# Moving the weight rings of a two-layer hybrid encoder into an on-chip pool of their own

## The chip, the cores and the metric

The kernel runs on one core of a Trainium2 chip. The metric is device time in microseconds of one execution, the median of several runs. The kernel before took 982.03 us (median of 3 runs, 981.92 to 982.07).

## The reference

Two layers work on an input x of 256 rows by 1024 columns, all in float32. Each layer has a mixing part with four branches (attention with compressed keys and values, a short convolution, a convolution of 31 taps, and a gated block) and a feed-forward part:

```python
for l in range(DEPTH):                       # DEPTH = 2
    h = rms_norm(x, norm_mix_pre[l])
    proj = h @ w_in[l]                       # 1024 x 8224
    (c_q, c_kv, k_rope, sc_b, sc_c, sc_x, cf_a, cf_g, gm_u, gm_v, gate_logits) = jnp.split(proj, pts, axis=-1)
    y_a = mla_branch(...) @ w_o_mla[l]
    y_b = short_conv_branch(...) @ w_o_sc[l]
    y_c = conformer_branch(...) @ w_o_cf[l]
    y_d = gmlp_branch(...) @ w_o_gm[l]
    g = jax.nn.sigmoid(gate_logits.reshape(B, S, N_BRANCH, D) + gate_b[l])
    merged = g[:, :, 0] * y_a + g[:, :, 1] * y_b + g[:, :, 2] * y_c + g[:, :, 3] * y_d
    x = x + rms_norm(merged @ w_out[l], norm_mix_post[l])
    h2 = rms_norm(x, norm_ffn_pre[l])
    f_g, f_u = jnp.split(h2 @ w_ffn_in[l], 2, axis=-1)       # 1024 x 5632
    x = x + rms_norm((jax.nn.silu(f_g) * f_u) @ w_ffn_out[l], norm_ffn_post[l])
```

All weights together are 41.4 million float32 numbers, each used for 256 rows.

## The kernel before

**Weights.** The host lays all weights out as a list of units in the order of their use, 128 partitions by at most 2048 numbers (`unit_list`). A unit passes through three rings of buffers. `Weights.load` (lines 325 to 334) takes a buffer `raw` (4 of them, 128 x 2048 float32) and issues its DMA on the SP queue. `Weights.split` (lines 336 to 351) takes a buffer `hi` and a buffer `lo` (5 of each, 128 x 2048 of the type F32R, four bytes a number): ScalarE copies `raw` into `hi`, which rounds it, and VectorE subtracts `hi` from `raw` into `lo`, in pieces of 1024 columns.

**Products.** The activations are split into a pair in the same way (`hth`/`htl` for the normalized input, `fh`/`fl`, `mh`/`ml` and others). A product of float32 precision is three matmuls: high with high, and high with low both ways (`group`, line 381). In most products `hi` and `lo` are the moving operand, up to 512 columns a matmul, and the activations are the stationary one, 128 columns loaded into the array before each matmul. In `b_unit` (12 units per layer) it is the other way round: 128 columns of `hi` or `lo` are loaded as the stationary operand and `hth` or `htl` is moving, 256 columns in two pieces of 128.

**Order.** A planner inside the program (`Engine`, `issue`, `event`, `pump`) simulates the engines with cost formulas and so writes out the order of the instructions of ScalarE, VectorE, GpSimd and SP once, when the program is built; matmuls are in the order of the text. It knows tiles by name and by offset inside the tile; where a tile lies in on-chip memory does not enter it.

**Pools and addresses.** Tiles come from pools (lines 256 to 258): `cp` for what lives throughout, `sb` for everything that rotates, and `ps` for PSUM. Pools lie one behind the other in the order in which they are opened; in a pool the rings (one per tag) lie one behind the other in the order of first use, each buffer rounded up to a multiple of 32 bytes per partition. The program's own list of buffers gives these starts, in bytes per partition:

| buffer | start | remainder by 64 |
|---|---|---|
| hth, htl (in cp) | 27,712, 35,904 | 0 |
| ident (in cp) | 24,768 | 0 |
| end of cp, first gain of sb | 44,096 | 0 |
| raw, 4 x 8192 | 52,288 and on | 0 |
| slots of 512 numbers (fh, mh, wst, gv, f, pt and others), 25 x 2048 | 85,056 and on | 0 |
| pii (2 numbers) | 136,256 | 0 |
| fr and others of 16 numbers | 136,288 | 32 |
| h, y: "big", 2 x 4096 | 136,544 | 32 |
| one-number columns, 8 x 32 | 144,736 | 32 |
| hi, 5 x 8192 | 144,992 and on | 32 |
| lo, 5 x 8192 | 185,952 and on | 32 |
| two-number columns | 226,912 | 32 |

The tile `pii` takes 32 bytes, and so all rings that follow it start 32 bytes past a multiple of 64. Within a unit, a column slice that a matmul reads starts at a multiple of 64 bytes from the start of its buffer (512, 1024, 1088, 1536 or 2048 bytes).

Of the kernel before, what the change touches and what calls it, by code (L numbers as in the profile page):

```python
# [11 lines left out]
F32 = mybir.dt.float32  # L12
F32R = mybir.dt.float32r
# [5 lines left out]
P = 128  # L19
# [14 lines left out]
UW = 2048  # L34
# [62 lines left out]
def hybrid_encoder(ctx: ExitStack, tc: tile.TileContext, wts, x_in, pos, invf, cols, rows, wst, out):  # L97
# [156 lines left out]
    act, dve, pool, sp, pe = Engine(nc.scalar, "ACT", cost_act), Engine(nc.vector, "DVE", cost_dve), Engine(nc.gpsimd, "POOL", cost_pool), Engine(nc.sync, "SP", lambda *a: 0.1), Tensor()  # L254

    cp = ctx.enter_context(tc.tile_pool(name="cp", bufs=1))
    sb = ctx.enter_context(tc.tile_pool(name="sb", bufs=1))
    ps = ctx.enter_context(tc.tile_pool(name="ps", bufs=1, space=bass.MemoryType.PSUM))

    B_RAW, B_HI, B_SLOT, B_BIG, B_GAIN = 4, 5, 25, 2, 2  # L260
# [7 lines left out]
    def nm(s):  # L268
        cnt[0] += 1
        return f"{s}_{cnt[0]}"  # L270
# [36 lines left out]
    def load(dst, src, after=0.0):  # L307
        nc.sync.dma_start(dst, src)  # L308
        n = 4.0 * width(dst) * dst.shape[0]
        dma[0] = max(dma[0], clock[0] + 1.0, after + 1.0) + n / 400e3  # L310
        mark(done, region(dst), dma[0] + 1.8)
# [8 lines left out]
    class Weights:  # L320
# [4 lines left out]
        def load(self, i, t=0.0):  # L325
            l, u = divmod(i, NU)
            w, after = widths[u], t
            t = sb.tile([P, UW], F32, tag="raw", name=nm("raw"), bufs=B_RAW)
            o = (l * offs[-1] + offs[u]) * P
            src = wts[o : o + w * P].rearrange("(p w) -> p w", w=w)  # L330
            step = FIRST if i == 0 else w
            for c in range(0, w, step):
                load(t[:, c : c + step], src[:, c : c + step], after)
            self.raw[i] = t

        def split(self, i):
            w = widths[i % NU]
            h = sb.tile([P, UW], F32R, tag="hi", name=nm("hi"), bufs=B_HI)
            lo = sb.tile([P, UW], F32R, tag="lo", name=nm("lo"), bufs=B_HI)
            raw = self.raw.pop(i)  # L340
            step = FIRST if i == 0 else 1024
            self.parts[i] = (h, lo)
            spans = [(c, min(w, c + step)) for c in range(0, w, step)]

            def rank():
                return 0 if i <= self.n + NEAR else 3

            for c, e in spans:
                act.copy(h[:, c:e], raw[:, c:e], rank=rank)
                dve.tensor_tensor(lo[:, c:e], raw[:, c:e], h[:, c:e], op=ALU.subtract, rank=rank, then=self.more if e == w else None)  # L350
# [54 lines left out]
    def gain(l, i):  # L405
        g = sb.tile([P, D], F32, tag="gain", name=nm("gain"), bufs=B_GAIN)
        load(g, rows[l : l + 1, i * D : (i + 1) * D].partition_broadcast(P))
        return g

    def brow(l, i):  # L410
        g = slot(s="brow")
        o = 4 * D + 512 * i
        load(g, rows[l : l + 1, o : o + 512].partition_broadcast(P))
        return g

    def gate_row(l, gi, n):
        g = slot(s="brow")
        o = 4 * D + 4 * 512 + D * gi + 512 * n
        load(g, rows[l : l + 1, o : o + 512].partition_broadcast(P))
        return g  # L420
# [54 lines left out]
    def pre_norm(t, g):  # L475
        h = big()
        ss = small(1)
        r = small(1)
        act.activation(h, x[:, t, :], AF.Square, scale=D ** -0.5, accum_out=ss, rank=FAST)
        rstd_of(r, ss, rank=FAST)  # L480
        for j in range(2):
            c = slice(512 * j, 512 * (j + 1))
            dve.scalar_tensor_tensor(h[:, c], x[:, t, c], r, g[:, c], op0=ALU.mult, op1=ALU.mult, rank=FAST)

        def turn():
            for j in range(2):
                yield need(h)
                b = sbank()
                transposes(b, [h[:, 512 * j + P * k : 512 * j + P * (k + 1)] for k in range(4)])
                bv = b.rearrange("p (k n) -> p k n", n=P)  # L490
                split(hth[:, t, 4 * j : 4 * j + 4, :], htl[:, t, 4 * j : 4 * j + 4, :], bv, FAST)

        return turn()
# [83 lines left out]
    def layer(l):  # L577
# [26 lines left out]
        def mla_tr(t, cn):  # L604
            yield need(cn)
            b = sbank()
            transposes(b, [cn[:, P * k : P * (k + 1)] for k in range(4)])
            for j in range(2):
                o = slice(t * P, (t + 1) * P)
                split(ft2(qc[j])[:, :, o], ft2(ql[j])[:, :, o], b[:, 256 * j : 256 * (j + 1)].rearrange("p (f n) -> p f n", f=2))  # L610
# [84 lines left out]
        def split_op(name, j, src):  # L695
            hi, lo = slot(F32R, name + "h"), slot(F32R, name + "l")
            split(hi, lo, src)
            ops[name][j] = (ft2(hi), ft2(lo))
# [481 lines left out]
```

## Time and profile before

| | us |
|---|---|
| median of 3 runs | 982.03 |
| the profiled execution | 981.91 |
| its span, first to last instruction | 980.1 |
| TensorE busy (matmuls) | 966.4 |
| VectorE busy | 670.3 |
| ScalarE busy | 476.2 |

The page of the profile shows the busy time of each engine, the chain of work that ended last, and the costliest groups of instructions. Matmuls overlap in the records: the next one starts while the last is still draining, so the recorded length of one (about 0.39 us for 512 columns) is not what it adds to the time. What it adds is the distance from its start to the next one's start; the chain shows it as the length of a piece divided by the number of its matmuls. Names of a matmul stand as output<-moving,stationary, followed by the size of the stationary operand and that of the output.

### The profile page before, as it was taken

What the parts mean: (1) busy time and instruction counts of PE and PEld (TensorE: products, weight loads), DVE (VectorE), ACT (ScalarE), POOL (GpSimd) and SP (SyncE); (2) the same over time, 40 slices, a digit from 0 to 9 for tenths busy, and PEclk for the clock granted to TensorE, in tenths of its full rate; (3) what the DMA queues carried; (4) which work ended last, traced back from release to release, by engine and by line L of the source; (5) the groups of instructions that cost most, each with busy time, mean ns of one, the idle gap of its engine ahead of it and who ended that gap; (6) DMA issues with size and microseconds to landing.
All of it is one profiled execution on the core that took longest, in us unless ns stands there. A gap on an engine that the chain in (4) does not pass through costs nothing.

```text
span 980.1 us, 12950 instructions
## 1 busy us (share of the span) xinstructions
PE 966.4 (99%) x5098; PEld 818.5 (84%) x5098; DVE 670.3 (68%) x1018; ACT 476.2 (49%) x733; POOL 44.5 (5%) x87
## 2 busy tenths in 40 slices
PE   8999999999999999999999999999999999999997
PEld 7999988888887888888899999888888878888885
DVE  6969888888847655553387888779987485544532
ACT  6666645345435544443275655444455364444421
POOL 1100000000001000000031000000000110000000
PEclk9999999999999999999999999999999999999999
DMA  9844344565744655464267244455576275555501
GB/s 363 290 154 172 121 170 151 183 216 189 282 150 172 220 191 190 172 217 175 86 238 279 78 172 168 142 174 203 183 258 222 77 261 212 172 178 192 211 0 43
DMA packets 29726, 179.52 MB, mean 183 GB/s; under 512 B 3681, under 2 KB 3809, under 8 KB 10209
## 3 DMA queue, kind: packets, MB, share of 16 engines
q1 hardware_dynamic: 29664, 178.69, 51.1%
q8 instruction: 40, 0.66, 0.3%
q14 instruction: 22, 0.17, 0.0%
HBM read 177.63 MB, written 1.05 MB: 182 GB/s over the span
## 4 chain that ended last, share of the span: by engine, by line
PE 94%; DVE 2%; ACT 1%; issue 1%; DMA 1%; POOL 1%; SPq 0%; DVEq 0%; POOLq 0%; ACTq 0%
PE pb L248 74%; PE acc L248 13%; PE psd L252 4%; PE psd L248 2%; PE av L248 1%; DVE lo L175 1%; DMA raw<-in_wts_dram 1%; POOL c L175 1%; ACT hi L175 1%; DVE h L175 0%; ACT h L175 0%; DVE x L175 0%; SPq L308 0%; DVE htl L175 0%; ACT sq L175 0%
## 5 line engine op out<-in xcount | busy, mean ns | idle before, releaser
L175 DVE TENSOR_TENSOR lo<-raw,hi 128x1024 fp32r<-128x1024 f32 (+4 forms) x321 | 374.1, 1202 | 142.4 <-ACT hi L175 141.9
L175 ACT CAST hi<-raw 128x1024 fp32r<-128x1024 f32 (+4 forms) x321 | 318.6, 1035 | 287.9 <-PE pb L248 153.8
L248 PE MATMUL pb<-hi,hth 128*128 128x512 f32 (+1 forms) x704 | 275.7, 392 | 1.0 <-ACT hth L175 1.0
L248 PE MATMUL pb<-lo,hth 128*128 128x512 f32 (+1 forms) x704 | 271.5, 386 | 3.3 <-DVE lo L175 3.3
L248 PE MATMUL pb<-hi,htl 128*128 128x512 f32 (+1 forms) x704 | 271.6, 386 | 0.6 <-DVE htl L175 0.4
L248 PEld LDWEIGHTS pb<-lo,hth 128*128 128x128 f32 x704 | 132.2, 188 | 32.0 <-DVE lo L175 4.6
L248 PEld LDWEIGHTS pb<-hi,htl 128*128 128x128 f32 x704 | 132.0, 187 | 31.0 <-DVE htl L175 2.0
L248 PEld LDWEIGHTS pb<-hi,hth 128*128 128x128 f32 x704 | 132.1, 188 | 28.7 <-ACT hth L175 1.3
L248 PE MATMUL pb<-hth,hi 128*128 128x256 f32 x384 | 109.2, 284 | 0.0
L248 PE MATMUL pb<-hth,lo 128*128 128x256 f32 x384 | 107.9, 281 | 0.0
L248 PE MATMUL pb<-htl,hi 128*128 128x256 f32 x384 | 107.9, 281 | 0.0
L175 DVE SCALAR_TENSOR_TENSOR yc<-zc,hcol,yc 128x241 f32<-128x241 f32 (+14 forms) x240 | 97.7, 471 | 0.0
L248 PEld LDWEIGHTS pb<-htl,hi 128*128 128x128 f32 x384 | 72.4, 189 | 0.3
L248 PEld LDWEIGHTS pb<-hth,hi 128*128 128x128 f32 x384 | 72.4, 188 | 0.3
L248 PEld LDWEIGHTS pb<-hth,lo 128*128 128x128 f32 x384 | 72.4, 188 | 0.0
L248 PE MATMUL acc<-hi,fh 128*128 128x512 f32 x176 | 69.8, 396 | 0.0
L248 PE MATMUL acc<-hi,fl 128*128 128x512 f32 x176 | 69.5, 395 | 0.0
L248 PE MATMUL acc<-lo,fh 128*128 128x512 f32 x176 | 69.5, 395 | 0.0
L248 PEld LDWEIGHTS acc<-hi,fl 128*128 128x128 f32 x176 | 33.0, 187 | 8.0
L248 PEld LDWEIGHTS acc<-hi,fh 128*128 128x128 f32 x176 | 33.0, 188 | 8.0
L248 PEld LDWEIGHTS acc<-lo,fh 128*128 128x128 f32 x176 | 33.0, 188 | 7.9
L175 POOL TENSOR_SCALAR c<-c 128x1 f32<-128x1 f32 (+1 forms) x20 | 12.5, 626 | 530.6 <-ACT sq L175 486.8
(161 smaller groups left out, 1009.9 us busy)
## 6 DMA issues: line engine op xcount, KB each, us to landing
raw<-in_wts_dram SPq DMA_DIRECT2D x152, 1024.0 KB, 4.8
brow<-in_rows_dram SPq DMA_DIRECT2D x24, 256.0 KB, 5.2
gain<-in_rows_dram SPq DMA_DIRECT2D x8, 512.0 KB, 6.2
raw<-in_wts_dram SPq DMA_DIRECT2D x3, 816.0 KB, 4.5
raw<-in_wts_dram SPq DMA_DIRECT2D x2, 768.0 KB, 5.9
raw<-in_wts_dram SPq DMA_DIRECT2D x2, 544.0 KB, 6.1
x<-in_x_dram SPq DMA_DIRECT2D x2, 512.0 KB, 5.9
out_dram<-x SPq DMA_DIRECT2D x4, 256.0 KB, 2.1
```

What stands on the lines that cost most here:

```text
L175: o.emit = lambda: f(*a, **k)
L248: nc.tensor.matmul(out, lhsT, rhs, **k)
L252: nc.tensor.transpose(out=out, in_=in_, identity=identity)
```

## The change

A third pool for on-chip memory, `wp`, is opened between `cp` and `sb`, and the three weight rings `raw`, `hi` and `lo` take their buffers from it in place of `sb`. Number, size, type and tags of the buffers stay; no instruction, wait or queue is named in the diff.

```diff
     cp = ctx.enter_context(tc.tile_pool(name="cp", bufs=1))
+    wp = ctx.enter_context(tc.tile_pool(name="wp", bufs=1))
     sb = ctx.enter_context(tc.tile_pool(name="sb", bufs=1))
...
         def load(self, i, t=0.0):
...
-            t = sb.tile([P, UW], F32, tag="raw", name=nm("raw"), bufs=B_RAW)
+            t = wp.tile([P, UW], F32, tag="raw", name=nm("raw"), bufs=B_RAW)
...
         def split(self, i):
             w = widths[i % NU]
-            h = sb.tile([P, UW], F32R, tag="hi", name=nm("hi"), bufs=B_HI)
-            lo = sb.tile([P, UW], F32R, tag="lo", name=nm("lo"), bufs=B_HI)
+            h = wp.tile([P, UW], F32R, tag="hi", name=nm("hi"), bufs=B_HI)
+            lo = wp.tile([P, UW], F32R, tag="lo", name=nm("lo"), bufs=B_HI)
```

## Rows read from the trace of the kernel before

**Rows 1.** The page, first part: busy time, share of the span and instructions of each engine.

```profile
PE 966.4 (99%) x5098; PEld 818.5 (84%) x5098; DVE 670.3 (68%) x1018; ACT 476.2 (49%) x733; POOL 44.5 (5%) x87
...
PEclk9999999999999999999999999999999999999999
```

**Rows 2.** The page, fourth part: the chain that ended last, by engine and by line.

```profile
PE 94%; DVE 2%; ACT 1%; issue 1%; DMA 1%; POOL 1%; SPq 0%; DVEq 0%; POOLq 0%; ACTq 0%
PE pb L248 74%; PE acc L248 13%; PE psd L252 4%; PE psd L248 2%; PE av L248 1%; DVE lo L175 1%; DMA raw<-in_wts_dram 1%; POOL c L175 1%; ACT hi L175 1%; DVE h L175 0%; ACT h L175 0%; DVE x L175 0%; SPq L308 0%; DVE htl L175 0%; ACT sq L175 0%
```

**Rows 3.** Waits of TensorE: who waited for whom, us in total, times, longest.

```profile
PE pb L248 <- DVE lo L175: 3.3, 3, 1.5
```

**Rows 4.** The chain in order of time, four pieces: start us, us, what, instructions.

```profile
350.82 22.39 PE pb L248 x96
...
432.25 57.39 PE acc L248 x246
...
592.97 5.68 PE pb L248 x48
```

**Rows 5.** TensorE in order of time, 506 to 512 us, first and last of 48: start, us, form.

```profile
506.05 0.29 PE L248 MATMUL pb<-hi,hth 128*128 128x272 f32 x1
...
511.94 0.29 PE L248 MATMUL pb<-hi,htl 128*128 128x272 f32 x1
```

**Rows 6.** Matmul groups by shape: count | busy us, mean ns of one | idle before.

```profile
L248 PE MATMUL pb<-hi,hth 128*128 128x512 f32 x640 | 257.0, 402 | 0.0
...
L248 PE MATMUL pb<-hi,hth 128*128 128x272 f32 x64 | 18.7, 292 | 1.0 <-ACT hth L175 1.0
...
L248 PE MATMUL pb<-hth,hi 128*128 128x256 f32 x384 | 109.2, 284 | 0.0
...
L248 PE MATMUL acc<-hi,fh 128*128 128x512 f32 x176 | 69.8, 396 | 0.0
...
L248 PE MATMUL pb<-hi,mh 128*128 128x512 f32 x64 | 25.8, 403 | 0.0
...
L248 PE MATMUL pb<-hi,sch 128*128 128x512 f32 x32 | 13.2, 412 | 0.0
```

**Rows 7.** Groups of weight loads on TensorE, same columns.

```profile
L248 PEld LDWEIGHTS pb<-hi,hth 128*128 128x128 f32 x704 | 132.1, 188 | 28.7 <-ACT hth L175 1.3
...
L248 PEld LDWEIGHTS pb<-hth,hi 128*128 128x128 f32 x384 | 72.4, 188 | 0.3
```

**Rows 8.** TensorE in order of time: eight transposes of h, and what starts after.

```profile
504.05 1.03 PE L252 MATMUL psd<-ident,h 128*128 128x128 f32 x8
504.92 0.60 PE L252 MATMUL psd<-ident,cn 128*128 128x128 f32 x4
```

**Rows 9.** The chain, columns as in rows 4: eight transposes of f; 16 records of psd<-wst,gv.

```profile
349.95 0.87 PE psd L252 x8
...
72.60 1.78 PE psd L248 x16
```

**Rows 10.** VectorE and ScalarE groups by shape, columns as in rows 6.

```profile
L175 DVE TENSOR_TENSOR lo<-raw,hi 128x1024 fp32r<-128x1024 f32 x311 | 368.6, 1220 | 142.4 <-ACT hi L175 141.9
...
L175 DVE TENSOR_TENSOR fl<-psd,fh 128x256 fp32r<-128x256 f32 x44 | 16.7, 418 | 6.0 <-PE pb L248 3.8 <-ACT fh L175 2.1
...
L175 DVE TENSOR_TENSOR m<-m,gt 128x512 f32<-128x512 f32 x24 | 16.4, 684 | 0.1
...
L175 ACT CAST hi<-raw 128x1024 fp32r<-128x1024 f32 x311 | 313.7, 1049 | 286.3 <-PE pb L248 153.8 <-issue 66.0 <-PE acc L248 38.0
L175 ACT ACTIVATE gt<-gt 128x512 f32<-128x512 f32 x32 | 18.7, 624 | 4.6 <-DVE gt L175 4.6
```

**Rows 11.** Two stretches: us, then busy us (count) of PE, PEld, DVE, ACT, POOL.

```profile
120.00:218.50 98.50, 98.50 (x495) 82.21 (x494) 84.56 (x141) 44.90 (x74) 2.10 (x6) 1.00 0.50 179
...
600.00:698.00 98.00, 98.00 (x493) 81.88 (x492) 83.65 (x141) 44.86 (x74) 2.10 (x6) 1.00 0.52 180
```

**Rows 12.** The page, DMA issues: out<-in, count, KB each, us to landing.

```profile
raw<-in_wts_dram SPq DMA_DIRECT2D x152, 1024.0 KB, 4.8
```

## The prediction

> **What bounds the kernel now.** I read the busy times first. [...] Busy time alone would be weak evidence, since an engine can be busy beside the work that sets the end; so the chain that ended last came second. It is 94% TensorE, and 87% of it are the two kinds of matmul that read the weights, `pb` and `acc`; VectorE's subtraction into `lo`, ScalarE's copy into `hi` and the DMA of `raw` have about 1% each [rows 2]. Third, the waits: matmuls that wait for `lo` lose 3.3 us in all [rows 3]. So the time is, nearly, the number of matmuls times the distance from one start to the next, and a change of addresses is worth something only if it changes that distance.
>
> The distances, fourth, from pieces of the chain that hold one kind of matmul. 96 matmuls of 512 columns in 22.39 us are 233.2 ns each, 246 of `acc` in 57.39 us are 233.3; 48 of 256 columns in `b_unit` in 5.68 us are 118.3 [rows 4]. From the first to the last of 48 matmuls of 272 columns lie 5.89 us, that is 47 distances of 125.3 ns [rows 5]. [...]
>
> **The change, part by part.** *What moves.* `wp` begins where `cp` ends, at 44,096 = 689 x 64. Its rings in order of first use: `raw` from 44,096, `hi` from 76,864 (1,201 x 64), `lo` from 117,824 (1,841 x 64); `sb` follows at 158,784 (2,481 x 64). `raw` lay at multiples of 64 before, so its DMAs [rows 12] and the reads of `raw` keep their alignment; of the 14 buffers only the ten `hi` and `lo` change it, from 32 to 0. What stays in `sb` keeps its remainder, since 14 x 8,192 bytes leave it. No instruction is added or removed, the planner sees no addresses, and so order, waits and queues (SP's too) should be those of before: cost 0.
>
> *Writes of `hi` and `lo`.* VectorE's subtraction takes 418 ns for 256 columns (`fl`) and 684 for 512 (`m`), both in slots at multiples of 64: 1.039 ns a column. Carried on to 1024 columns that is 684 + 512 x 1.039 = 1,216; `lo`, at 32, takes 1,220 [rows 10]. Misaligned writing costs VectorE 4 ns at most, 311 x 4 ns = 1.2 us, and next to nothing of that is on the path. For ScalarE the rows have no such ladder; twice the 624 ns of `gt` is more than the 1,049 of `hi` [rows 10], which excludes no more than a doubling. The cover for both is the five buffers of each ring: TensorE hardly ever waits for them [rows 3]. I take 0, bounds -2 to +1 us.
>
> *Reads as the moving operand: the term that decides.* Here the trace holds a comparison. `hi` is read at 32 past 64 in the matmuls of 512 and 272 columns; `hth`, which lies at 0, is the moving operand of those with 256. If the excess grows by the column, whatever the start, then from 272 to 512 a column costs (233.3 - 125.3) / 240 = 0.450 ns and 2.9 ns are fixed, and 256 aligned columns give 2.9 + 256 x 0.450 = 118.1. [...] Measured: 118.3 [rows 4, 5]. The aligned operand pays the same excess per column as the misaligned one. I take 0 here.
>
> The comparison has one hole. In `b_unit` it is the stationary operand that is `hi`, at 32, so 118.3 could be the pace of a misaligned weight load. Two rows speak against that. Loads of `hi` (at 32) are recorded with 188 ns, loads of `hth` (at 0) with 188 as well [rows 7]; 10% on the part that streams would show. And eight transposes take 0.87 us whether the loaded tile is `h`, at 32, or `f`, at 0 [rows 8, 9]. But these are no loads of F32R weights at their limit, so the hole isn't quite closed. [...]
>
> The sum: 981.91 us of the profiled execution (its span 980.1 and 1.8 around it, 0.1 under the median) plus 0 for order and waits, 0 for the writes, 0 for the reads.
>
> [...]
>
> **The rivals.** [...]
>
> [...]
>
> *Same start for both operands, slower.* Before, every matmul with weights reads one operand from 32 and the other from 0. Afterwards both start at a multiple of 64, and if the two reads get in each other's way there, each matmul pays. The nearest row with both at 0 is the products with `wst` and `gv`, 1.78 us / 16 = 111.3 ns a record, beside 108.8 for a transpose of as many columns [rows 8, 9]: 2.5 ns. Times 4,368 matmuls that is 10.9 us: 993 us. It decides from any collision above 0.5 ns on. Against: transposes of `f`, with both operands at 0, are as fast as those of `h`. That the change does not do what it says is in part the forecast: for `raw` there is nothing to align.
>
> **How the numbers follow.** This kernel's times differ by 0.02% between runs, and about 0.2% (2 us) is what a comparison can tell from no change. Forecast 982.0 us, within 0.2%: 0.68, with a range of its own of 980 to 983. One block less, about 959: 0.14. The whole excess, 906 to 929: 0.08. A small gain of 2 to 10 us from parts of either: 0.03. Slower by the collision, 984 to 993: 0.07. Faster is 0.14 + 0.08 + 0.03 = 0.25. The range of 957 to 984 leaves out the whole excess and most of the slower case, some 0.14.
>
> **What would show it.** Right: the pieces of the chain keep 233 ns for 512 columns, 125 for 272 and 118 for 256, and `lo` keeps about 1,220 ns. [...] The collision: all three distances longer by the same few ns. The prediction is wrong if any of these distances moves by over 0.5 ns; if they stay and the time moves, the order of the instructions or a wait has changed after all.

## The result and the profile after

| | before | after |
|---|---|---|
| median, us (4 runs each, side by side) | 982.05 | 966.65 |
| lowest to highest | 981.92 to 982.12 | 966.32 to 966.78 |
| ratio after/before, 95% interval | | 0.9843 (0.9828 to 0.9858) |
| the profiled execution | 981.91 | 966.32 |
| its span | 980.1 | 964.5 |

The kernel became 15.4 us or 1.6% faster. The forecast of 982.0 with "no change" as the likeliest case was wrong; the time lies inside the range of 957 to 984.

The first parts of the page of the kernel after (busy time, share, instructions; then the granted clock of 40 slices, then the chain that ended last by engine and by line):

```profile
PE 950.7 (99%) x5098; PEld 821.9 (85%) x5098; DVE 669.5 (69%) x1018; ACT 476.4 (49%) x733; POOL 44.6 (5%) x87
...
PEclk9999999999999999999999999999999999999999
...
PE 94%; DVE 2%; ACT 1%; issue 1%; DMA 1%; POOL 1%; SPq 0%; DVEq 0%; POOLq 0%; ACTq 0%
PE pb L248 74%; PE acc L248 12%; PE psd L252 4%; PE psd L248 2%; PE av L248 1%; DVE lo L175 1%; DMA raw<-in_wts_dram 1%; POOL c L175 1%; ACT hi L175 1%; DVE h L175 0%; ACT h L175 0%; DVE x L175 0%; SPq L309 0%; DVE htl L175 0%; ACT sq L175 0%
```

Beside [rows 1, 2] one number has moved by much: TensorE is busy for 15.7 us less, in a span that is 15.6 us shorter (its loads are recorded 3.4 us longer in all). Counts, clock and, but for one per cent at `acc`, the make-up of the chain are those of before. Laid side by side, the two traces have the same operations on the same tiles in the same order on every engine. So the work is the same, it waits for nearly the same things, and TensorE goes through it faster.

Where, the chain in order of time says (start us, us, what, instructions; the 113 us row is a `b_unit` stretch of layer 0, the last one of layer 1):

```profile
112.71 5.74 PE pb L248 x48
...
369.35 21.78 PE pb L248 x96
...
425.99 55.81 PE acc L248 x246
...
585.60 5.75 PE pb L248 x48
```

Against [rows 4]: 96 matmuls of 512 columns take 21.78 us, 226.9 ns from start to start, where it was 233.2; 246 of `acc` take 55.81, again 226.9 for 233.3. In `b_unit`, 48 of 256 columns take 5.75 us, 119.8 ns for 118.3: these became slower. The 272-column stretch, TensorE in order of time (first and last of 48):

```profile
498.10 0.29 PE L248 MATMUL pb<-hi,hth 128*128 128x272 f32 x1
...
504.02 0.29 PE L248 MATMUL pb<-hi,htl 128*128 128x272 f32 x1
```

5.92 us for 47 distances, 126.0 ns beside the 125.3 of [rows 5]. The 512-column matmuls gained 6.3 ns or 2.7% each; beside them only the 48 of 384 columns gained, from 175.0 to 173.7 ns. Adding up all start-to-start distances on TensorE by shape, from the starts in the two traces, gives the account of the whole difference (us):

```
shape                         before    after    change
512 columns (3,072)            725.0    707.6     -17.4
256 columns, b_unit (1,152)    137.6    139.4      +1.8
272 columns (192)               27.3     27.5      +0.1
all others                                         -0.2
sum                                               -15.6
```

(The prediction counted 4,368 matmuls in all: it left out one product (`cth`, `ctl`) with 48 of 512 and 48 of 384 columns. The trace has 3,072 and 4,464.) 3,072 x 6.3 ns would be 19.4 us; the difference from 17.4 lies in matmuls that follow a wait or another kind of matmul and don't run at the steady pace.

The side terms: waits of TensorE (who for whom, us, times, longest), the groups of `lo` and `hi` by shape, two groups of matmuls, TensorE's weight loads, and the window where VectorE is fullest (us, then busy us and count of PE, PEld, DVE, ACT, POOL), all of after:

```profile
PE pb L248 <- DVE lo L175: 3.9, 3, 1.5
```

```profile
L175 DVE TENSOR_TENSOR lo<-raw,hi 128x1024 fp32r<-128x1024 f32 x311 | 368.6, 1220 | 136.3 <-ACT hi L175 136.1
...
L175 ACT CAST hi<-raw 128x1024 fp32r<-128x1024 f32 x311 | 314.1, 1052 | 275.7 <-PE pb L248 140.6 <-issue 64.1 <-PE acc L248 36.3
...
L248 PE MATMUL pb<-hi,hth 128*128 128x512 f32 x640 | 253.8, 397 | 0.0
...
L248 PE MATMUL pb<-hth,hi 128*128 128x256 f32 x384 | 109.9, 286 | 0.0
...
L248 PEld LDWEIGHTS pb<-hi,hth 128*128 128x128 f32 x704 | 132.3, 188 | 24.8 <-ACT hth L175 1.1
...
L248 PEld LDWEIGHTS pb<-hth,hi 128*128 128x128 f32 x384 | 73.6, 192 | 0.3
```

```profile
120.00:218.00 98.00, 98.00 (x504) 83.60 (x503) 84.83 (x142) 46.25 (x77) 2.10 (x6) 1.00 0.51 182
```

`lo` takes 1220 ns as before and `hi` 1052 for 1049 [rows 10]: the aligned writes gained nothing. Waits for `lo` are 3.9 us for 3.3 [rows 3], VectorE works 84.8 of 98.0 us [rows 11], so TensorE still sets the pace. Loads of `hi` in `b_unit` read 192 ns for 188 [rows 7], while the other loads keep 188. The recorded lengths of matmuls moved with the pace, but by less: 397 for 402 ns at 512 columns, 286 for 284 at 256 [rows 6].

### The profile page after: what moved, and what is told of

The parts are those of the page before. It is cut to its first block, busy times and chain, and to the rows that moved or that the text cites. A ratio compares the mean times of both kernels' runs of the same rounds, so it can differ in the third digit from the quotient of the medians.

```text
span 964.5 us, 12950 instructions
## 1 busy us (share of the span) xinstructions
PE 950.7 (99%) x5098; PEld 821.9 (85%) x5098; DVE 669.5 (69%) x1018; ACT 476.4 (49%) x733; POOL 44.6 (5%) x87
## 4 chain that ended last, share of the span: by engine, by line
PE 94%; DVE 2%; ACT 1%; issue 1%; DMA 1%; POOL 1%; SPq 0%; DVEq 0%; POOLq 0%; ACTq 0%
PE pb L248 74%; PE acc L248 12%; PE psd L252 4%; PE psd L248 2%; PE av L248 1%; DVE lo L175 1%; DMA raw<-in_wts_dram 1%; POOL c L175 1%; ACT hi L175 1%; DVE h L175 0%; ACT h L175 0%; DVE x L175 0%; SPq L309 0%; DVE htl L175 0%; ACT sq L175 0%
## 5 line engine op out<-in xcount | busy, mean ns | idle before, releaser
L248 PE MATMUL pb<-hi,hth 128*128 128x512 f32 (+1 forms) x704 | 272.5, 387 | 0.8 <-ACT hth L175 0.8
L248 PE MATMUL pb<-lo,hth 128*128 128x512 f32 (+1 forms) x704 | 268.1, 381 | 3.9 <-DVE lo L175 3.9
L248 PE MATMUL pb<-hi,htl 128*128 128x512 f32 (+1 forms) x704 | 268.3, 381 | 0.7 <-DVE htl L175 0.4
```

What stands on the lines that cost most here:

```text
L248: nc.tensor.matmul(out, lhsT, rhs, **k)
```

## The experiments

Two theories stood at the start and a third came to them; each run carries what they expect of it. **A**: what counts is whether the moving operand starts at a multiple of 64 bytes. **B**: what counts is whether both operands have the same remainder by 64. **C**, formed after the first four runs: what counts is the difference between the starts of the loaded and the moving operand, by a period longer than 64. The place of each buffer is from the program's own list; "512" and "256" below are steady distances from start to start of matmuls with so many columns. The kernel before, on the same chips, took 982.01 to 982.12 us.

**All at 32 past a multiple of 64** (`w32_a32`): `hi` and `lo` in buffers 64 bytes wider, read from their ninth number on; the same for `hth` and `htl`, and small tiles of 32 bytes ahead of the slots and behind them.

```diff
-            h = wp.tile([P, UW], F32R, tag="hi", name=nm("hi"), bufs=B_HI)
+            h = wp.tile([P, UW + 16], F32R, tag="hi", name=nm("hi"), bufs=B_HI)[:, 8 : 8 + UW]
...
+    sb.tile([P, 8], F32, tag="pad0", name="pad0")
...
-    hth = cp.tile([P, T, KD, P], F32R, name="hth")
+    hth = cp.tile([P, T * KD * P + 16], F32R, name="hth")[:, 8 : 8 + T * KD * P].rearrange("p (t k n) -> p t k n", t=T, k=KD)
...
```

> hi and lo are put back to 32 bytes past a multiple of 64, and the activation pairs (hth, htl and all slots) are moved there too, so that both operands of every weight matmul start at 32. Theory A (the start of the moving operand alone decides): matmuls of 512 columns go back to 233.3 ns, those of 272 to 125.2, and the whole stays near 982 us. Theory B (it decides whether the two operands start at the same remainder by 64): 512 columns 226.9 ns, 256 columns in b_unit 119.9, the whole near 966.7 us as in the changed kernel.

**Weights at multiples of 64, activations at 32** (`w0_a32`): the `hth`, `htl` and pad lines of the diff above alone, with `hi` and `lo` as in the kernel after.

> hi and lo stay at multiples of 64 as in the changed kernel, and the activation pairs (hth, htl and all slots) move to 32 past one. Theory A (start of the moving operand): 512 columns stay at 226.9 ns, only b_unit, where hth is moving, changes; the whole within about 5 us of 966.7. Theory B (same remainder): 512 columns 233.3 ns, 272 columns 125.2, 256 columns 118.4 as before, the whole near 982 us.

**Only `lo` at 32** (`hi0_lo32`): as in the first diff, but for `lo` alone.

> One part of the change alone: hi at a multiple of 64, lo at 32 past one, activations at 0. Both theories: of the three matmuls the two with hi as the moving operand take 226.9 ns at 512 columns and the one with lo 233.3, the whole near 973 us (a third of the gain given back). If lo or hi alone carried the effect by way of their writers, it would be 966.7 or 982. In b_unit theory A expects the same distance for all three (moving is hth or htl), theory B 118.4 where lo is the loaded operand and 119.9 where hi is.

**`hi` and `lo` 16 bytes past** (`w16`): `[:, 4 : 4 + UW]` in place of `[:, 8 : 8 + UW]`, activations as in the kernel after.

> hi and lo start 16 bytes past a multiple of 64, activations at 0. If every start off a multiple of 64 costs the same (theory A as a step, or theory B with any difference), 512 columns take 233.3 ns and the whole is near 982 us. If the cost grows with the distance from the multiple of 64, it lies half way, near 230 ns and 974 us. If only 32 and more matter, 226.9 ns and 966.7 us.

Measured: 978.65, 979.24, 978.41 and 978.78 us. The chains (one piece of 512 columns each, in this order):

```profile
373.32 22.30 PE pb L248 x96
```

```profile
373.39 22.19 PE pb L248 x96
```

```profile
373.30 22.29 PE pb L248 x96
```

```profile
373.18 22.26 PE pb L248 x96
```

231 to 232 ns in all four, neither the 233.3 of before nor the 226.9 of after. `w0_a32` has every weight at a multiple of 64 and is slow, which A doesn't allow; `w32_a32` has equal remainders by 64 and is slow, which B doesn't allow. Both fell, and so did my expectation for `hi0_lo32` (973 us); `w16` met none of its three cases. Three of these runs have a flaw of mine: a buffer of 8,256 bytes moves the next one by 64, so the five buffers of a ring no longer share a remainder by larger powers of two, and one run mixes several cases. Sorted by the difference between the two operands' starts, the mean 512-column distances of `w16` run from 230.4 to 233.2 ns; that suggested C. The cleanest is `w0_a32`, whose weight buffers have one remainder: the weights start 192 past a multiple of 512, `hth` 96, `htl` 160 and the slots 224 past, and nowhere is the difference zero.

**Everything moved together by 32** (`w96_a96`): one tile of 32 bytes ahead of `hth`, so all rings behind it, `raw` among them, lie 32 past multiples of 64, and all differences stay.

```diff
+    cp.tile([P, 8], F32, name="padc")
     hth = cp.tile([P, T, KD, P], F32R, name="hth")
```

> The changed kernel with 32 bytes of padding ahead of hth, so that raw, hi, lo, hth, htl and all slots move together to 96 past a multiple of 512, that is 32 past a multiple of 64 (in the changed kernel all lie at 64 past a multiple of 512). Theory A (multiples of 64 decide): 512 columns 233 ns, near 982 us. Theory B (same remainder by 64 for both operands) and theory C (same remainder by a longer period, 512): 226.9 ns, 256 columns 119.9, near 966.7 us.

Measured: 966.54 us, beside 966.65 of after. Its chain:

```profile
369.64 21.78 PE pb L248 x96
...
426.29 55.81 PE acc L248 x246
...
585.87 5.75 PE pb L248 x48
```

To the digit the pieces of after, with no operand of these matmuls at a multiple of 64. This settles that alignment to 64 bytes isn't what brought the gain.

**Weights 64 bytes further, all at multiples of 64** (`w128_a64`): a pad ahead of the rings and one behind them, so `sb` keeps its remainder.

```diff
+            if i == 0:
+                wp.tile([P, 112], F32, tag="pade", name="pade")
...
+    wp.tile([P, 16], F32, tag="padw", name="padw")
```

> The changed kernel with raw, hi and lo moved by 64 bytes more: all buffers still begin at multiples of 64, but the weights lie at 128 and the activations at 64 past a multiple of 512. Theories A and B: nothing changes, 226.9 ns for 512 columns, near 966.7 us. Theory C: 231 to 234 ns, near 978 to 982 us.

Measured: 967.90 us.

```profile
111.85 5.66 PE pb L248 x48
...
392.91 21.99 PE pb L248 x96
...
427.22 56.31 PE acc L248 x246
...
584.86 5.46 PE pb L248 x48
```

Both paces move, in opposite directions: 512 from 227.1 to 229.1 ns, 256 from 119.9 to 116.1 in the mean (117.9 in the first piece shown, 113.8 in the last), with every start at a multiple of 64. A and B expected no change in either. C had the direction for 512, but its 978 to 982 us was too much: it took any difference but zero to cost the full price.

**Five differences in one kernel, steps of 64** (`scan64`): each of the five buffers of `hi`, and likewise of `lo`, 64 bytes further than the one ahead of it.

```diff
-            h = wp.tile([P, UW], F32R, tag="hi", name=nm("hi"), bufs=B_HI)
+            h = wp.tile([P, UW + 16], F32R, tag="hi", name=nm("hi"), bufs=B_HI)[:, :UW]
+            if i == 0:
+                wp.tile([P, 48], F32, tag="padm", name="padm")
...
```

> The five buffers of hi and of lo lie 0, 64, 128, 192 and 256 bytes past the activations' remainder by 512, the same for the hi and the lo of one unit, so that all matmuls of a unit have one difference. Theories A and B: all five buffers give 226.9 ns for 512 columns, near 966.7 us. Theory C: only the buffers with difference 0 give 226.9, the others 229 to 235; the whole between 975 and 981 us. It also shows whether some difference is better than 0, for 512 columns or for the 256 of b_unit.

**The same in steps of 32** (`scan32`): `UW + 8`, and 88 for 48.

> As scan64, with buffers 0, 32, 64, 96 and 128 bytes past the activations' remainder by 512. Theory C: for 512 columns 227 ns at 0, 233.3 at 32 (as in the kernel before), 229.1 at 64 (as in w128_a64), 232 at 128 (as in scan64), and at 96 something between 229 and 234, not 227; the whole near 975 us.

Measured: 974.24 us, a little under the expected 975 to 981, and 976.79 us; the chains show only the mixture (230.5 and 232.1 ns), first `scan64`, then `scan32`:

```profile
371.71 22.13 PE pb L248 x96
```

```profile
372.36 22.28 PE pb L248 x96
```

Sorted by buffer, with the runs whose buffers share a remainder beside them (loaded operand's start minus the moving one's, remainder by 256; means in ns from start to start, where the difference stays the same from matmul to matmul):

```
difference   512 columns                           256 columns
0            227.1 after; scan64 229.0, 228.0*;    119.9 after; scan64 119.9, 120.0*
             scan32 228.1
32           w0_a32 233.3                          118.3 before; scan32 118.3
64           scan64 233.3                          116.1 w128_a64; scan64 116.0; scan32 115.7
96                                                 scan32 118.4; w0_a32 117.8
128          scan64 232.3; scan32 232.7            scan64 118.6; scan32 118.6
160          scan32 233.6; w0_a32 231.9
192          w128_a64 229.1; scan64 229.5;         scan64 116.6
             scan32 229.8
224          before 233.3; scan32 233.1
* with a difference of 256
```

The kernel before stands in this table at 224 for 512 columns and at 32 for 256, the kernel after at 0 for both. The operand that was called aligned in the prediction has nothing special about it. A difference of 256 is as good as none (in `scan64` 228.0 ns beside 229.0 for 512 columns, 120.0 beside 119.9 for 256), so the period is 256 bytes, for both shapes. 512 columns have their best at 0 (226.9 ns in the chain of after); for 256 columns 0 is the worst (119.9). The matmuls of 272 columns fit in: their slices lie 1,088 bytes apart, so within a unit the difference runs through four values by 256. In the kernel after they take 127.3 ns at 0, 124.1 at 64, 126.1 at 128 and 124.7 at 192, in the kernel before 124.0 to 125.8 at 32, 96, 160 and 224. Zero is the worst again, and the mean hardly changes. Three limits of the table: the 256-column means at 64 and 192 mix two paces, told apart under `best64`; the same difference can give about 2 ns less in another run (160 in `w0_a32`, where every third matmul has a difference of 224, so that other starts and the alternation can't be told apart), and it holds for a difference that lasts. In the scans, where units of other differences follow each other, zero reads 228 to 229 with 231 and 236 mixed in; in `w32_a32` and `hi0_lo32`, where it changes from one matmul to the next, matmuls of 512 columns at zero take 232.9 and 231.9 ns on average. What goes before a matmul counts too, then, and C is a rule for a steady stream, not for one matmul.

**The pool kept, the difference of before restored** (`w96_a64`): 32 bytes ahead of the rings in `wp`.

```diff
+            if i == 0:
+                wp.tile([P, 120], F32, tag="pade", name="pade")
...
+    wp.tile([P, 8], F32, tag="padw", name="padw")
```

> The changed kernel with 32 bytes of padding at the start of the new pool: own pool and all, but raw, hi and lo at 96 past a multiple of 512, the activations at 64, the difference of the kernel before. Theory C (the difference between the two operands' starts decides): 233.3 ns for 512 columns, 118.3 for 256, near 982 us. If the pool itself, that is the distance of the rings from the other buffers, is the cause: 226.9 ns, near 966.7 us.

Measured: 982.02 us beside 982.11 of before, and its chain is [rows 4] again:

```profile
374.22 22.39 PE pb L248 x96
...
432.38 57.39 PE acc L248 x246
...
593.11 5.68 PE pb L248 x48
```

So the pool as such gives nothing; 32 bytes against the activations are the whole of the 15.4 us. The pair of `w96_a96` and `w96_a64` says it most simply: the weights lie at 96 in both, the activations at 96 in the one (966.54 us) and at 64 in the other (982.02).

**Half the columns loaded** (`halfload`): is the price paid by each column that is loaded (theory L), or is it one fixed amount per load (theory F)? In the down projection all but the first and last three matmuls of a bank load 64 of the 128 columns, so half of the output rows are left unsummed.

```diff
+                    if not (st or sp):
+                        o, lh, ll = o[:64, :], lh[:, :64], ll[:, :64]
```

> The changed kernel, in which the matmuls of the last product (acc, w_ffn_out), but for the first and last 128 rows' worth of each bank, load 64 stationary columns in place of 128 and so write only 64 of the 128 rows of the output: that part of the product is left out for the other rows. [...] Theory F (a fixed price of each such matmul): 226.9 ns as with the full load.

Measured: 968.29 us. The untouched part, the changed part, and its loads (form, count, busy us, mean ns):

```profile
369.75 21.78 PE pb L248 x96
...
426.39 56.59 PE acc L248 x246
```

```profile
L248 PEld LDWEIGHTS acc<-hi,fh 128*64 128x64 f32 x160 | 21.5, 134 | 14.7
```

Loads fall from 188 to 134 ns, and the distance rises from 226.9 to 230.0 (irregular, 224 to 236). A price by the column loaded (L) would make the distance shorter, one per load (F) leave it at 226.9: both miss. The price isn't in proportion to what is loaded, and it isn't indifferent to it; the edit also halves the output rows that a matmul writes, and the run doesn't separate the two. A stream of matmuls without loads was not tried, and the mechanism stays open.

**A version made from the table** (`best`): for 512 columns a difference of 0 or 256, for `b_unit` 64. Buffers of 8,448 bytes (33 x 256) keep the remainder, and the units of `b_unit` lie 64 bytes further in theirs. To make room, the halved taps are written in place and some small rings have fewer buffers.

```diff
-            h = wp.tile([P, UW], F32R, tag="hi", name=nm("hi"), bufs=B_HI)
-            lo = wp.tile([P, UW], F32R, tag="lo", name=nm("lo"), bufs=B_HI)
+            o = 16 if units[i % NU][0] == "w_in" and w == 8 * 256 and units[i % NU][2] - units[i % NU][1] == D else 0
+            h = wp.tile([P, UW + 64], F32R, tag="hi", name=nm("hi"), bufs=B_HI)[:, o : o + UW]
+            lo = wp.tile([P, UW + 64], F32R, tag="lo", name=nm("lo"), bufs=B_HI)[:, o : o + UW]
```

> A version that takes the best difference for each kind of matmul. hi and lo get buffers of 8448 bytes, so that all keep the activations' remainder by 256, and the units of b_unit are put 64 bytes further in their buffers, so that there the loaded operand lies 64 bytes past the moving one. Room for it comes from the halved taps, written over the first ones in place, and from fewer small buffers. Theory C: 512 columns stay at 227.1 ns, 256 columns go from 119.9 to 116.1; 1152 x 3.8 ns = 4.4 us, so near 962.2 us. If the period were 512 rather than 256, every second buffer would lose the gain and the time would lie above 966.7.

Measured: 963.18 us (962.68 to 964.39, 5 runs), ratio to before 0.9808 (0.9794 to 0.9821): 3.5 us below the kernel after. Its chain:

```profile
368.70 21.78 PE pb L248 x96
...
425.35 55.82 PE acc L248 x246
...
583.91 5.66 PE pb L248 x48
```

512 keeps 226.9 ns in the chain, now in buffers with differences of 0 and of 256 alike (227.1 in both), which shows the period without the scans' mixture. 256 goes to 117.7, not to the 116.1 of `w128_a64`, and the time misses the expected 962.2 us by 1.0; the halved taps and the smaller rings were not run by themselves. In `w128_a64` the weights lay at 128 by 256 and the activations at 64; without the 992 bytes of the taps' second copy, `hth` starts at 96 and the weights of `b_unit` at 160.

**The same with `hth` 32 bytes further** (`best64`): `best` and the `padc` line, so that all starts are multiples of 64 again, with the same differences.

> The version with the best difference for each kind of matmul, with 32 bytes of padding ahead of hth, so that activations and weights start at 128 past a multiple of 256 in place of 96, and the units of b_unit at 192 in place of 160. In the version without the padding the 256 columns took 117.7 ns, in w128_a64 and in the scans, where the activations lay at 64, 116.1 with the same difference of 64 bytes. If the difference between the two operands alone decides, nothing changes: 117.7 ns, 963.2 us. If the start itself counts too (a multiple of 64 or not) where the two operands differ, 116.1 ns, 1152 x 1.6 = 1.8 us less, near 961.4 us.

```profile
368.14 21.81 PE pb L248 x96
...
424.88 55.80 PE acc L248 x246
...
582.16 5.46 PE pb L248 x48
```

In this trace 256 has a mean of 116.6 at a difference of 64 and 115.2 at 320. But these are mixtures of two paces. Unit by unit, 8 of the 24 units of `b_unit` run at 113.3 to 113.8 ns and 16 at 117.6 to 117.8; in `w128_a64` it is 9 and 15, in `best` none and 24. In `w128_a64` the same buffer (start 76,928) has units of both paces, so it isn't the start that picks one, and these runs don't show that the start counts. In time `best64` can't be told apart from `best`: 963.75 us (962.58 to 963.87), ratio 0.9812 (0.9798 to 0.9825), and not the 961.4 expected if the start counts. The trace of `best` is of its slowest execution (964.39 us), that of `best64` of its fastest (962.58), and 8 x 48 x 4.5 ns = 1.7 us is nearly all that lies between the two. What picks the pace of a unit, and whether it changes from one execution to the next, stays open.

## Why the prediction was wrong, and where it was right

The sign that the prediction set itself, any distance moved by over 0.5 ns, came: 512 columns moved by 6.3 ns and 256 by 1.5.

**What bounds the kernel: right.** TensorE's distances set the time, and the change of the distances is the change of the time (15.6 us in the trace by either count).

**What moves, and order, waits, queues at 0: right.** The operations are the same in the same order, and `w96_a64` gives 982.02 with the new pool. `raw` counts for nothing: in `w96_a96` it lies at 32 past 64 and the time stays at 966.54.

**Writes at 0: right,** 1220 ns before and after for `lo`, 1049 and 1052 for `hi`.

**Reads as the moving operand, taken at 0: the step that failed.** It measured -15.6 us: -17.4 for 512 columns, +1.8 for 256, +0.1 for 272, -0.2 for the rest. The comparison set 118.3 ns for an aligned moving operand against a line through 125.3 and 233.3 for misaligned ones, found them on that line, and read from it that the start doesn't matter. The base from which the prediction counts its excess is shown by no run; the line does without it (0.450 ns a column from 272 to 512). But the two sides don't differ in what matters. With 512 columns the loaded operand lay 32 bytes below the moving one (by the remainder), with 256 columns 32 above: the same gap, by 64, in each F32R matmul of the trace. None has the gap 0 that the change brings, so the trace could not size this term. By 256 the 125.3 ns of 272 columns are a mean over four differences besides, and the line was drawn through it. The hole that the text named (in `b_unit` it is the loaded operand that is misaligned) was the right place to look; what was wrong was to take it as nearly closed by the recorded lengths of loads and by transposes. The lengths of loads scarcely speak: 188 ns at 226.9 and at 233.3 ns alike. And the transposes and the products with `wst` are float32. In the kernel after they keep their pace ([rows 9] have 0.87 and 1.78), but there the difference of their own starts is also that of before (128 for transposes of `f`, 0 for `wst`), so this tests nothing. The chain of after, eight transposes of `f` and 16 records of `wst`:

```profile
345.82 0.87 PE psd L252 x8
```

```profile
72.75 1.78 PE psd L248 x16
```

The test is in other runs, where the transposes of `f` have a difference of 0 (`w16`), 32 (`w0_a32`) and 192 (`hi0_lo32`) and still take 0.87 us, in this order:

```profile
349.18 0.87 PE psd L252 x8
```

```profile
349.45 0.87 PE psd L252 x8
```

```profile
349.26 0.87 PE psd L252 x8
```

So to the 0.01 us that the chain shows for eight, these float32 transposes don't react to what F32R matmuls react to, and couldn't close the hole. The products with `wst` have a difference of 0 in every run; whether they react is not shown.

The fit was also finer than its rows. The distances of before are means over 231, 233, 234 and 235 ns for 512 columns and over 116 to 122 for 256; that scatter, which steady distances of 226 and 227 in the kernel after don't have, was in the trace, and the fit passed over it.

**One block less, about 959 us: not shown.** No run shows a price for a block of bytes that a matmul touches. In `w96_a96` `hi` and `lo` start 32 past a multiple of 64, as they did before, and 512 columns take 226.9 ns, where before they took 233.3.

**The whole excess, 906 to 929 us: wrong.** No run shows the pace that this excess is counted from, or a time near these: the lowest steady distance of 512 columns is 226.9 ns, the shortest execution 962.58 us (`best64`). What the kernel after shows in its place are 226.9 ns for 512 columns and 119.9 for 256, that is (226.9 - 119.9) / 256 = 0.418 ns a column and 12.9 ns fixed.

**Same start for both operands, slower, 993 us: the right quantity with the wrong sign.** It was the only case that spoke of how the two starts stand to each other. At equal starts 256 columns do pay, 1.5 ns x 1,152 = 1.7 us, but 512 columns gain 6.3. The price was taken from float32 matmuls with `wst`, whose two starts never moved against each other in any run.

**The chances.** 0.68 for no change rested on a comparison of five numbers from one and the same arrangement. The range held, since it reached down past the 959 us of one block less. That 966.65 us fell inside is luck as far as the mechanism goes: no case stood for it. It lies between a small gain of at most 10 us and the 959 us of one block less, for whose price no run speaks.

## What to carry to other kernels

In a stream of F32R matmuls that each load new weights, look up the starts of the loaded and of the moving operand per partition, and place the rings so that their difference is a multiple of 256 bytes for 512-column matmuls (here 226.9 ns for 233.3); for 256 columns try 64 (115.7 to 117.7 ns in the mean, for 119.9; the best version here: 963.2 us for 966.65). A pad of some tens of bytes does it, and the number that shows it is the distance from start to start in a piece of the chain with one kind of matmul; the recorded lengths of loads don't show it (188 ns before and after at 512 columns) and those of matmuls only in part (397 ns for 402). The gain was seen with `hi` and `lo` in F32R in this kernel alone. Before a comparison inside a trace is taken as evidence that something costs nothing, write down for both sides every quantity that the change moves, relations between operands included: what is equal on both sides isn't tested.

## What was not expected of the hardware

The pace of an F32R matmul depends on where its two operands lie to each other: in a steady stream 226.9 to 233.6 ns for 512 columns and 113.3 to 120.0 for 256, with a period of 256 bytes, at a granted clock of 0.996 to 0.999 in all runs. The best place for 512 columns, a difference of zero, is the worst for 256. There 256, 384 and 512 columns take 119.9, 173.7 and 226.9 ns, nearly on one line: 0.418 ns a column from 256 to 512 and 12.9 ns fixed, which gives 173.4 for 384. At the starts of before the same three took 118.3, 175.0 and 233.3. Between `w96_a64` (982.02 us) and `w96_a96` (966.54) the weights keep their place at 96; what differs is where the activations lie to them. Why it is so, why the matmuls before one count, and why a load of half the columns made matmuls of 512 columns 3 ns slower (230.0 for 226.9 ns in `halfload`), remains open.
